# Two-layer trunk on one core: the sums of weight blocks formed in the second MLP sweep, the rotary tables beside the first gates, and softmax with priority

## The chip, the core and the metric

The kernel runs on one core of a Trainium2 chip. A core has a tensor engine (PE in the profile), a vector engine (DVE), a scalar engine (ACT), GpSimd (POOL), and a sync engine (SP) which here only issues transfers. Each engine takes its instructions in order from a queue of its own; semaphores make one engine wait for another. The metric is the device time in microseconds (us) of one execution, lower is better.

## The reference

One sequence of 1024 tokens, width 1024, passes two layers, all in float32. Layer 0 is an mLSTM mixer (8 heads, chunks of 128 tokens) and an MLP. Layer 1 is multi-head latent attention (8 heads, causal, rotary part of 64 columns) on keys and values made once from a low-rank latent, and an MLP. Every norm's gain and shift is modulated by vectors made from the condition `c` through large matrices (`ada_w`, `kv_ada_w`).

```python
def rope_tables(positions):
    half = B_ROPE // 2
    inv = ROPE_THETA ** (-jnp.arange(half, dtype=jnp.float32) / half)
    ang = positions.astype(jnp.float32)[..., None] * inv
    return jnp.cos(ang), jnp.sin(ang)
...
    for l in range(DEPTH):
        ada = cond @ ada_w[l] + ada_b[l]
        sh1, sc1, g1, sh2, sc2, g2 = jnp.split(ada, 6, axis=-1)
        h = modulate(rmsnorm(x, norm_g[l, 0]), sh1, sc1)
        if l < N_A:
            y = mlstm_mixer(h, a_w_in[l], a_gate_b[l], a_head_g[l], a_w_out[l])
        else:
            ...
            y = mla_mixer(h, b_w_q_a[j], b_q_latent_g[j], b_w_q_b[j], b_w_out[j],
                          k_nope, k_rope, v, cos, sin)
        x = x + g1[:, None, :] * rmsnorm(y, norm_g[l, 1])
        h = modulate(rmsnorm(x, norm_g[l, 2]), sh2, sc2)
        y = sqrelu_mlp(h, mlp_w1[l], mlp_w2[l])
        x = x + g2[:, None, :] * rmsnorm(y, norm_g[l, 3])
```

## The kernel before

**Products.** Each float32 operand is split into a rounded high part and a rest; a product is three matmuls (`mm3`, lines 280 to 282: high by high, high by rest, rest by high). A weight tile of 128x1024 is loaded by SP into one of four `raw` buffers; `wsplit` (lines 238 and 239) makes the high part on ACT and the rest on DVE, both in `ws` buffers. So each weight that PE takes has been a transfer, an ACT and a DVE instruction before.

**Order.** The program is traced as generators (`yield` marks a place where another strand may be woven in). A scheduler then sets the order on every engine by an estimate of its own; `prompt` (high priority) lets a piece go ahead of other ready work. `tc.issue_after` ties some DVE work to a point. What counts for this page is the resulting order on each engine, which is shown below where the change moves it.

**Buffers.** Tiles come from rings: `k4` (24 buffers of 128x1024), `hd` (8), `raw` (4), `ws` (8), `tmp` (3), `tmc` (6), and in the accumulators of PE `ps` (2), `pc` (2), `pm` (2 double ones). An instruction that takes a ring's next buffer waits until its last user is done.

**Stages,** by the trace: to 69 us the first half's input, its modulation and its query and key products; from 77 us the first gates (`gates_in`, `gates0`); up to about 510 us the mLSTM of both halves. Then the first MLP. It multiplies by blocks: the tokens are two halves, the weight `w1` is cut in halves along both sides, and seven block products stand in for eight. `Mlp.sweep1` (510 to 690 us) makes the products of the plain blocks, `sweep2` (690 to 893 us, `second`) those of sums and differences of blocks for the first half's results, and `sweep3` (from 893 us, `third`) the rest, beside `attention_first`, the attention of the first half. Afterwards come the second half's attention and the second MLP.

**Block sums.** For each of 16 column blocks `p_`, four 128x512 sums of `w1` blocks are wanted. `block_sums` makes all of them early: GpSimd's queue loads two tiles of 512 KB (line 2578), DVE makes four sums (lines 2583 to 2587), GpSimd's queue stores two tiles of 512 KB in the scratch tensor `t0` (lines 2585 and 2588). Five of the sixteen are woven into the first gates and the last query and key products (buffers `hd`), one more into what follows, and the rest into the second half's mLSTM. `second` reads two quarters of `t0` and one raw quarter of `w1`, and `third` reads the other two quarters. `self.made` says for which `p_` this holds: all sixteen of layer 0.

**Modulation and latents.** `ada_chunk` (lines 377 to 384) loads four tiles of 512 KB and adds them up on DVE, eight instructions of 128x512. In the first MLP a strand `behind(bg_latent(), 5)` walks beside the sweeps: the rest of these chunks, then `rope_tables` (sine and cosine of position by frequency, in two halves of 512 columns, range reduction on GpSimd, sines on ACT), then `latent_weights`, six weight tiles scaled and split. A `yield "wait"` ends the strand's turn until the next step of the sweep.

**First attention.** `attention_first` makes keys and query of a head (`kq`), the rotary part (`rot`), the values (`val`) and, in `scores` and `softmax` (lines 1832 to 1836: maximum, scaling on DVE, exponential on ACT, reciprocal and scaling on DVE), the weights, which PE then transposes (lines 1942 and 1953) for the product with the values.

## Time and profile before

| | |
|---|---|
| three runs | 2375.53, 2379.48, 2379.86 us; median 2379.48 |
| the profiled execution | 2381.42 us, of which the profile's span is 2379.6 |
| PE busy | 2298.5 us, 97% of the span |
| DVE busy | 1709.8 us, 72% |
| ACT busy | 1128.1 us, 47% |
| POOL busy | 160.7 us, 7% |
| moved by transfers | 465.37 MB, a mean of 196 GB/s |

The span is cut by stages in what follows. Of a stage, the reader wants four numbers: how long PE was not busy, at what clock it ran (1.00 is the full clock), how full DVE was, and how full the transfer engines were.

### The profile page before, as it was taken

Reading aid. Unit: us, or ns where it says so; the run is one execution under the profiler, and the core shown is the slowest. Engines: PE = TensorE matmul, PEld = TensorE weight load, DVE = VectorE, ACT = ScalarE, POOL = GpSimd, SP = SyncE. Lnnn points to the kernel's source line nnn. Section 1 sums busy time; section 2 is a strip of 40 time slices with the busy share of each in tenths; the row PEclk is TensorE's granted clock in tenths of the full one; section 3 lists DMA queues with packets and bytes.
Section 4 is the critical chain, followed back from the end, with each engine's and each line's share of the span. In section 5 each row is a group of like instructions: output and inputs, shape, how many; then the busy total and the mean of one; then the engine's idle time right before and its main releaser. Section 6 shows DMA issues by size and latency. Waiting matters only on the chain.

```text
span 2379.6 us, 32796 instructions
## 1 busy us (share of the span) xinstructions
PE 2298.5 (97%) x12042; PEld 1932.3 (81%) x12042; DVE 1709.8 (72%) x2771; ACT 1128.1 (47%) x1913; POOL 160.7 (7%) x271
## 2 busy tenths in 40 slices
PE   7899999999999999999899999999999999999998
PEld 5788797787778888777788778888888888999997
DVE  6576777889976766776674777766566478788776
ACT  3255433566435545543444555444444445555543
POOL 2100003103621100000000000000000000000000
PEclk9999999999999999999999999999999999999999
DMA  9862478956887967565576855683432452455432
GB/s 344 278 178 81 135 213 256 356 195 214 262 285 246 299 215 269 180 225 182 174 229 188 268 168 178 212 287 131 158 109 103 147 162 82 134 169 163 133 107 107
DMA packets 390594, 465.37 MB, mean 196 GB/s; under 512 B 27971, under 2 KB 265600, under 8 KB 390432
## 3 DMA queue, kind: packets, MB, share of 16 engines
q1 hardware_dynamic: 371136, 394.47, 52.7%
q0 software_dynamic: 19296, 68.79, 8.1%
q8 instruction: 95, 1.56, 0.3%
q14 instruction: 67, 0.55, 0.1%
HBM read 356.23 MB, written 106.95 MB: 195 GB/s over the span
## 4 chain that ended last, share of the span: by engine, by line
PE 66%; DVE 7%; DMA 5%; ACT 3%; issue 2%; SPq 1%; DVEq 0%; POOL 0%; ACTq 0%; POOLq 0%
PE ps L282 10%; PE ps L280 10%; PE ps L281 10%; PE pm L280 8%; PE pm L281 8%; PE pm L282 8%; PE pc L281 2%; PE pc L282 2%; PE pc L280 2%; DMA raw<-in_mlp_w_dram 2%; DVE tma L384 1%; PE pc L2023 1%; DVE wl L239 1%; DMA raw<-in_ada_w_dram 1%; DVE k L247 1%
## 5 line engine op out<-in xcount | busy, mean ns | idle before, releaser
L238 ACT CAST wh<-raw 128x1024 fp32r<-128x1024 f32 (+5 forms) x323 | 327.9, 1017 | 490.3 <-PE ps L281 170.3
L239 DVE TENSOR_TENSOR wl<-raw,wh 128x1024 fp32r<-128x1024 f32 (+5 forms) x323 | 383.2, 1188 | 242.2 <-ACT wh L238 198.5
L280 PE MATMUL ps<-k,wh 128*128 128x512 f32 (+1 forms) x1228 | 466.9, 380 | 5.5 <-ACT k L682 1.7
L282 PE MATMUL ps<-k,wl 128*128 128x512 f32 (+1 forms) x1228 | 460.1, 375 | 2.0 <-DVE wl L239 2.0
L281 PE MATMUL ps<-k,wh 128*128 128x512 f32 (+1 forms) x1228 | 459.8, 374 | 0.0
L280 PEld LDWEIGHTS ps<-k,wh 128*128 128x128 f32 x1228 | 232.0, 189 | 50.4 <-issue 2.6
L282 PEld LDWEIGHTS ps<-k,wl 128*128 128x128 f32 x1228 | 231.9, 189 | 45.0 <-DVE wl L239 3.4
L281 PEld LDWEIGHTS ps<-k,wh 128*128 128x128 f32 x1228 | 232.1, 189 | 40.9 <-issue 1.7
L247 DVE TENSOR_TENSOR k<-k,pm 128x512 f32<-128x512 f32 (+1 forms) x250 | 192.3, 801 | 79.2 <-PE pm L282 78.6
L280 PE MATMUL pm<-wh,hd 128*128 128x512 f32 x488 | 193.4, 396 | 3.0 <-ACT raw L1834 1.8
L281 PE MATMUL pm<-wl,hd 128*128 128x512 f32 x488 | 190.4, 390 | 0.0
L282 PE MATMUL pm<-wh,hd 128*128 128x512 f32 x488 | 190.4, 390 | 0.0
L384 DVE SCALAR_TENSOR_TENSOR tma<-raw,cond,tma 128x512 f32<-128x512 f32 x168 | 131.9, 785 | 17.0 <-DMA raw<-in_ada_w_dram 11.9
L280 PEld LDWEIGHTS pm<-wh,hd 128*128 128x128 f32 x488 | 91.7, 188 | 24.8 <-ACT raw L1834 4.5
L282 PEld LDWEIGHTS pm<-wh,hd 128*128 128x128 f32 x488 | 91.6, 188 | 19.7 <-DVE hd L494 0.5
L280 PE MATMUL pc<-k,wh 128*128 128x256 f32 (+1 forms) x316 | 103.4, 327 | 3.9 <-DVE hd L494 3.9
L1834 ACT ACTIVATE raw<-pm,sm 128x128 f32<-128x128 f32 (+3 forms) x64 | 47.5, 742 | 125.0 <-DVE sm L1833 122.8
L281 PEld LDWEIGHTS pm<-wl,hd 128*128 128x128 f32 x488 | 91.7, 188 | 18.4 <-issue 0.5
L280 PE MATMUL pm<-hd,wk 128*128 128x512 f32 x256 | 101.6, 397 | 2.2 <-ACT hd L493 2.2
L281 PE MATMUL pc<-k,wh 128*128 128x256 f32 (+1 forms) x316 | 103.4, 327 | 0.2 <-DVE k L494 0.2
L282 PE MATMUL pc<-k,wl 128*128 128x256 f32 (+1 forms) x316 | 103.2, 327 | 0.0
L281 PE MATMUL pm<-hd,wk 128*128 128x512 f32 x256 | 101.0, 395 | 1.9 <-DVE hd L494 1.9
(496 smaller groups left out, 4921.1 us busy)
## 6 DMA issues: line engine op xcount, KB each, us to landing
raw<-in_mlp_w_dram SPq DMA_DIRECT2D x144, 512.0 KB, 4.3
raw<-in_ada_w_dram SPq DMA_DIRECT2D x80, 512.0 KB, 5.2
raw<-in_mlp_w_dram SPq DMA_DIRECT2D x144, 256.0 KB, 4.4
raw<-in_a_w_in_dram SPq DMA_DIRECT2D x44, 512.0 KB, 5.2
lo<-wl POOLq DMA_DIRECT2D x32, 512.0 KB, 6.1
raw<-t SPq DMA_DIRECT2D x64, 256.0 KB, 5.1
wk<-lo SPq DMA_DIRECT2D x64, 256.0 KB, 4.3
k<-in_mlp_w_dram POOLq DMA_DIRECT2D x22, 512.0 KB, 9.8
```

The lines of the kernel that those rows point to most:

```text
L238: nc.scalar.copy(hi[:, :n], r[:, :n])
L239: i = nc.vector.tensor_sub(lo[:, :n], r[:, :n], hi[:, :n].bitcast(F32))
L247: return f(*a, **k)
L280: nc.tensor.matmul(o, lh, rh, start=start, stop=False)
L281: nc.tensor.matmul(o, lh, rl, start=False, stop=False)
L282: pe_last[0] = nc.tensor.matmul(o, ll, rh, start=False, stop=stop)
L384: nc.vector.scalar_tensor_tensor(acc, r[:, kk], cond[:, k : k + 1], acc, ALU.mult, ALU.add)
L1834: nc.scalar.activation(pr[:, :n], f, AF.Exp, bias=m, scale=SCALE, accum_out=l)
L2023: nc.tensor.transpose(pt[:, ts(2 * e + i, P)], u.prs[i][:, ts(b + e, P)], ident)
```

## The change

Three things change.

1. `block_sums`, `t0`, `order` and `made` go. `second` loads the two `w1` tiles of a block itself, and makes the three sums it needs on DVE and the fourth on GpSimd; a tile `s` with the two sums that `third` wants is stored by GpSimd's queue. `third` loads it as one tile.
2. `rope_tables` moves from the strand beside the sweeps to a place before `gates_in` of the first half. It works on all 1024 columns at once, in three `hd` tiles, with nearly all its arithmetic on GpSimd and its transfers on GpSimd's queue. It starts when the modulation's shift of the first norm is known (the one-column copy into `d`). `latent_weights` ends its turn two or three times a tile instead of once.
3. In `attention_first` the query's product takes its accumulator from `ps` instead of `pc`; `rot` goes ahead of the next even head's `kq`; `softmax` has priority in both attentions.

```diff
@@ class Mlp @@
-            self.made = not l and order or []
@@ second, load @@
-                if p_ in self.made:
-                    r = [raw(), raw()]
-                    nc.sync.dma_start(r[0][:, l_], t0[p_][:, 0:512])
-                    nc.sync.dma_start(r[1][:, l_], t0[p_][:, 1024:1536])
-                    nc.sync.dma_start(
-                        r[1][:, r_].rearrange("p (a b) -> p a b", b=P),
-                        wcols(self.w1, (p_ + NPR) * P, P, 4, 4),
-                    )
...
                 r = [raw(), raw()]
                 for i in range(2):
                     nc.sync.dma_start(
...
                 w = wsplit(r[1], 1024)
-                nc.vector.tensor_sub(o[:, r_], r[0][:, r_], r[0][:, l_])
+                nc.gpsimd.tensor_sub(o[:, r_], r[0][:, r_], r[0][:, l_])
                 nc.gpsimd.dma_start(self.s[p_], o)
@@ third, load @@
-                if p_ in self.made:
-                    nc.sync.dma_start(r[:, 0:512], t0[p_][:, 1536:2048])
-                    nc.sync.dma_start(r[:, 512:1024], t0[p_][:, 512:1024])
-                else:
-                    nc.sync.dma_start(r, self.s[p_])
+                nc.sync.dma_start(r, self.s[p_])
@@ latent_weights @@
-            yield "wait"
+            for _ in range(3 if b == 0 else 2):
+                yield "wait"
@@ scores, twice @@
-                softmax(st[:, e, :n], pr[:, e], n, e == 0)
+                prompt(softmax)(st[:, e, :n], pr[:, e], n, e == 0)
@@ attention_first @@
-            for t, k0, n, of, alloc in ((kt, 0, 2, hf.ckv, ps), (q, 2, 3, hf.cq, pc)):
+            for t, k0, n, of, alloc in ((kt, 0, 2, hf.ckv, ps), (q, 2, 3, hf.cq, ps)):
...
-                work += [kq(2 * p_ + 2), rot(p_ + 1), val(p_ + 1)]
+                work += [rot(p_ + 1), kq(2 * p_ + 2), val(p_ + 1)]
@@ rope_tables, new place @@
+        d, a, kf = hd(), hd(), hd()
+        pi = d.bitcast(I32)
+        nc.gpsimd.tensor_copy(d[:, 0:1], adac(0, SH1)[:, 7:8])
+        nc.gpsimd.dma_start(pi, positions.to_broadcast([P, S]))
+        nc.gpsimd.tensor_copy(a, pi)
+        nc.gpsimd.tensor_scalar(a, a, inv, None, ALU.mult)
+        yield
+        nc.gpsimd.tensor_scalar(kf, a, 1.0 / (2.0 * PI), MAGIC, ALU.mult, ALU.add)
+        nc.gpsimd.tensor_scalar_add(kf, kf, -MAGIC)
+        for part in TWO_PI_PARTS:
+            yield
+            nc.gpsimd.tensor_scalar(d, kf, -part, None, ALU.mult)
+            nc.gpsimd.tensor_add(a, a, d)
+        yield
+        nc.gpsimd.tensor_scalar(a, a, 3.1415925, -3.1415925, ALU.min, ALU.max)
+        nc.vector.scalar_tensor_tensor(kf, a, -1.0, a, ALU.mult, ALU.max)
+        nc.vector.tensor_scalar(kf, kf, -1.0, PI / 2, ALU.mult, ALU.add)
+        nc.scalar.activation(d, a, AF.Sin)
+        last = nc.scalar.activation(kf, kf, AF.Sin)
...
+        nc.gpsimd.tensor_scalar(d, d, sg, None, ALU.mult)
+        nc.gpsimd.dma_start(rope_d[1], d)
+        nc.gpsimd.dma_start(rope_d[0], kf)
@@ the program @@
-    pre = block_sums()
-    at_prep[0] = hd
-    drain(with_bg(with_bg(gates_in(hfs[0]), bgs, 1), pre, 1))
-    drain(with_bg(with_bg(qk_last(hfs[0]), bgs, 1), pre, 1))
+    drain(rope_tables())
+    drain(with_bg(gates_in(hfs[0]), bgs, 1))
+    drain(with_bg(qk_last(hfs[0]), bgs, 1))
...
-    drain(weave_n(with_bg(with_bg(main, bgs, 1.5), pre, 0.2), intra0(hfs[1]), 0.95))
+    drain(weave_n(with_bg(main, bgs, 1.5), intra0(hfs[1]), 0.95))
@@ bg_latent @@
         yield from bgs
-        yield from rope_tables()
```

The scheduler's order moves with this at three places. The first is DVE's queue at the end of the first query and key products. The names `hd` are the tiles of the block sums, `k` with L497 the rests of the modulated input that PE multiplies next, `wl` the rest of a weight. Before:

```order
L2381 SCALAR_TENSOR_TENSOR tmc_477<-k_14_148,mods,Cst 128x512
L2583 TENSOR_TENSOR hd_665<-hd_665 128x512
L2584 TENSOR_TENSOR hd_665<-hd_664,hd_665 128x512
L239 TENSOR_TENSOR wl_480<-raw_412,wh_479 128x1024
L2368 TENSOR_TENSOR ada<-pc_489,cols 128x4
L2586 TENSOR_TENSOR hd_664<-hd_665,hd_664 128x512
L2583 TENSOR_TENSOR hd_739<-hd_739 128x512
L2587 TENSOR_TENSOR hd_664<-hd_664 128x512
L497 SCALAR_TENSOR_TENSOR k_46_235<-tmc_475,ada,k_45_234 128x512
```

And with the change:

```order
L2327 SCALAR_TENSOR_TENSOR tmc_476<-k_14_147,mods,Cst 128x512
L239 TENSOR_TENSOR wl_479<-raw_411,wh_478 128x1024
L2314 TENSOR_TENSOR ada<-pc_488,cols 128x4
L497 SCALAR_TENSOR_TENSOR k_46_234<-tmc_474,ada,k_45_233 128x512
L497 SCALAR_TENSOR_TENSOR k_46_234<-tmc_476,ada,k_45_233 128x512
```

The block sums no longer stand between the modulation and the rests. GpSimd's queue has the rotary tables there in place of the block sums' transfers; these rows of it, with the change, show the memset of L730 (a tile that `gates0` fills for the decay matrices) behind a part of the tables:

```order
L2526 COPY hd_610<-ada 128x1
L2527 DMA hd_610<-in_positions_dram 128x1024
L625 MEMSET tmc_670 128x8x24
L2528 CAST hd_611<-hd_610 128x1024
L2529 TENSOR_SCALAR hd_611<-hd_611,inv 128x1024
```

```order
L2536 TENSOR_TENSOR hd_611<-hd_611,hd_610 128x1024
L730 MEMSET tmc_840 128x512
L2535 TENSOR_SCALAR hd_610<-hd_612 128x1024
L2536 TENSOR_TENSOR hd_611<-hd_611,hd_610 128x1024
L2535 TENSOR_SCALAR hd_610<-hd_612 128x1024
L2536 TENSOR_TENSOR hd_611<-hd_611,hd_610 128x1024
```

The second place is DVE in the second sweep. L247 are PE's results added up, L239 and L1030 (L1031 with the change) rests of weights, L1622 and L1624 (L1567 and L1569) the bias of a latent tile. Before, one step of the sweep:

```order
L247 TENSOR_TENSOR k_1218_7090<-k_1218_7090,ps_7225 128x512
L1624 SCALAR_TENSOR_TENSOR tma_7188<-raw_7186,ada,tma_7188 128x128 x5
L247 TENSOR_TENSOR k_1218_7090<-k_1218_7090,pc_7239 128x512
L239 TENSOR_TENSOR wl_7206<-raw_7186,wh_7205 128x1024
L1030 TENSOR_TENSOR wv_7218<-raw_7211,wv_7218 128x512
L247 TENSOR_TENSOR tmp_7255<-k_1218_7090,ps_7254 128x512
L239 TENSOR_TENSOR wl_7222<-raw_7212,wh_7221 128x1024
L239 TENSOR_TENSOR wl_7278<-raw_7274,wh_7277 128x1024
L494 TENSOR_TENSOR hd_7269<-tmp_7255,hd_7269 128x512
L247 TENSOR_TENSOR k_805_4784<-k_805_4784,pm_7282 128x1024
```

With the change, a step without a latent tile:

```order
L1026 TENSOR_TENSOR k_1202_7035<-raw_7031 128x512
L247 TENSOR_TENSOR k_1185_6932<-k_1185_6932,ps_7049 128x512
L1027 TENSOR_TENSOR raw_7031<-raw_7030,raw_7031 128x512
L1028 TENSOR_TENSOR raw_7030<-k_1202_7035,raw_7030 128x512
L247 TENSOR_TENSOR k_1185_6932<-k_1185_6932,pc_7063 128x512
L1031 TENSOR_TENSOR wv_7040<-raw_7030,wv_7040 128x512
L239 TENSOR_TENSOR wl_7044<-raw_7031,wh_7043 128x1024
L239 TENSOR_TENSOR wl_7102<-raw_7098,wh_7101 128x1024
L247 TENSOR_TENSOR tmp_7079<-k_1185_6932,ps_7078 128x512
L494 TENSOR_TENSOR hd_7093<-tmp_7079,hd_7093 128x512
L247 TENSOR_TENSOR k_776_4665<-k_776_4665,pm_7106 128x1024
```

Three sums (L1026 to L1028) stand among the accumulations; a latent tile's work now stands in every second step, and before it stood in consecutive ones. The third place is ACT in the first attention, around the second exponential of a unit with 512 keys (L1834, L1780 with the change). Before:

```order
L1834 ACTIVATE raw_9295,sm_9309<-pm_9294,sm_9308 128x384
L493 CAST k_1604_9331<-pc_9341 128x512
L238 CAST wh_9326<-raw_9323 128x640
L1834 ACTIVATE raw_9295,sm_9317<-pm_9294,sm_9316 128x512
L974 ACTIVATE u_1563_9134<-u_1563_9134 128x512
```

With the change:

```order
L1780 ACTIVATE raw_9172,sm_9186<-pm_9171,sm_9185 128x384
L493 CAST k_1579_9208<-ps_9218 128x512
L1780 ACTIVATE raw_9172,sm_9194<-pm_9171,sm_9193 128x512
L238 CAST wh_9203<-raw_9200 128x384
L974 ACTIVATE u_1538_9013<-u_1538_9013 128x512
```

The cast of a weight that has to be loaded first now stands behind the exponential.

More of the change, by code (lines that the diff above doesn't have):

```diff
@@ L1858, in scores @@
                 pr = raw()
-                softmax(st.rearrange("p a b -> p (a b)")[:, :n], pr, n, e == 0)
+                prompt(softmax)(st.rearrange("p a b -> p (a b)")[:, :n], pr, n, e == 0)
                 prs.append(pr)
@@ L2628 @@
             )
-    pre = block_sums()
-    at_prep[0] = hd
-    drain(with_bg(with_bg(gates_in(hfs[0]), bgs, 1), pre, 1))
-    drain(with_bg(with_bg(qk_last(hfs[0]), bgs, 1), pre, 1))
+    drain(rope_tables())
+    drain(with_bg(gates_in(hfs[0]), bgs, 1))
+    drain(with_bg(qk_last(hfs[0]), bgs, 1))
     x1 = load_x1()
-    at_prep[0] = k4
-    for _ in range(2):
-        next(pre, None)
     drain(weave(with_bg(v_in(hfs[0]), bgs, 1), intra0(hfs[0]), 2.5))
```

71 lines of the change are left out of this document (12 added, 59 removed).

## The prediction

> **What bounds the kernel now.** I read the page first, then PE's busy time by stages, then PE's longest waits, then the engines around each wait. The page says that PE is nearly always busy, and that the transfer engines are full in places (first row the vector of 40 slices, then totals).
>
> ```profile
> span 2379.6 us, 32796 instructions
> PE 2298.5 (97%) x12042; PEld 1932.3 (81%) x12042; DVE 1709.8 (72%) x2771; ACT 1128.1 (47%) x1913; POOL 160.7 (7%) x271
> DMA  9862478956887967565576855683432452455432
> ```
>
> So a change that leaves PE's products as they are can win only PE's 81 us of idle time (2379.6 - 2298.5) and the time that PE runs below its full clock. The stages show where both lie; the columns are the stretch, its length, each engine's busy time, PE's granted clock, the transfer engines' share and GB/s.
>
> ```profile
> 40.00:90.00 50.00, 36.90 (x179) 30.66 (x172) 28.97 (x43) 12.77 (x25) 11.24 (x21) 0.80 0.98 336
> 380.00:480.00 100.00, 90.17 (x413) 72.81 (x412) 82.42 (x145) 48.96 (x87) 23.82 (x41) 0.95 1.04 336
> 590.00:690.00 100.00, 89.65 (x380) 70.72 (x380) 92.70 (x111) 44.36 (x59) 52.38 (x46) 0.97 0.83 276
> 690.00:900.00 210.00, 210.00 (x934) 173.61 (x933) 140.27 (x206) 100.05 (x157) 23.99 (x47) 1.00 0.79 255
> 1020.00:1200.00 180.00, 162.65 (x837) 135.70 (x836) 123.22 (x246) 72.66 (x144) 2.95 (x13) 0.96 0.61 192
> ```
>
> Idle time: 13.1, 9.8, 10.4, 0 and 17.4 us. The first two stages hold block sums and full transfer engines, the third the rotary tables, the fifth the first attention; the fourth, the second sweep, has no gap and is where the change puts work.
>
> **The first products and gates (40 to 90 us).** DVE waits for a block sum's transfer, and the rest that PE needs (L497) stands behind the sums; PE then waits, and later once more for the gates' weights.
>
> ```profile
> 42.72 0.69 DVE L2583 TENSOR_TENSOR hd<-hd 128x512 f32<-128x512 f32 x1 [1.74 <-DMA hd<-in_mlp_w_dram]
> ...
> 48.35 0.69 DVE L2583 TENSOR_TENSOR hd<-hd 128x512 f32<-128x512 f32 x1 [1.35 <-DMA hd<-in_mlp_w_dram]
> 48.97 0.68 DVE L2587 TENSOR_TENSOR hd<-hd 128x512 f32<-128x512 f32 x1
> 49.57 0.74 DVE L497 SCALAR_TENSOR_TENSOR k<-tmc,ada,k 128x512 fp32r<-128x512 f32 x1
> ```
> ```profile
> 47.22 0.80 PE L280 MATMUL pm<-k,wh 128*128 128x512 f32 x1 [3.05 <-ACT k L496]
> 50.36 0.80 PE L281 MATMUL pm<-k,wh 128*128 128x512 f32 x1 [2.35 <-DVE k L497]
> ...
> 77.10 0.59 PE L280 MATMUL ps<-wh,k 128*128 128x272 f32 x1 [7.71 <-ACT k L247]
> ```
> ```profile
> 72.42 1.65 ACT L238 CAST wh<-raw 128x816 fp32r<-128x816 f32 x2 [15.24 <-DMA raw<-in_a_w_in_dram]
> ```
>
> The block tiles on GpSimd's queue (ten here, 22 later; KB each and median us to landing):
>
> ```profile
> k<-in_mlp_w_dram POOLq DMA_DIRECT2D x22, 512.0 KB, 9.8
> ...
> hd<-in_mlp_w_dram POOLq DMA_DIRECT2D x10, 512.0 KB, 10.1
> ```
>
> After each gap PE ran at half clock for some us, as these short stretches show.
>
> ```profile
> 77.00:83.40 6.40, 6.30 (x28) 6.30 (x29) 6.37 (x12) 0.99 (x5) 1.84 (x7) 0.51 0.97 342
> 47.00:56.00 9.00, 6.43 (x14) 4.75 (x15) 7.65 (x13) 3.21 (x5) 1.07 (x2) 0.50 1.03 350
> 392.00:400.00 8.00, 7.13 (x42) 6.04 (x43) 5.74 (x11) 1.25 (x3) 3.45 (x5) 0.67 1.03 328
> 455.00:470.00 15.00, 10.65 (x39) 7.88 (x38) 15.00 (x23) 12.90 (x22) 1.05 (x7) 0.89 1.05 349
> ```
>
> Without block sums DVE reaches L497 after one weight rest instead of five further instructions. *Term A*: the gaps are 3.05 + 2.35 = 5.4 us, the clock costs 6.43 x 0.50 = 3.2 us, 8.6 in all; some 2 us of the gap belong to the weight and the modulation themselves, so I take -6 (bounds -8.6 and 0). *Term B*: the gates' weights come late because the queue is full: ten block tiles, 5 MB, and as much in stores share it. The gap is 7.7 us and the clock costs 6.30 x 0.49 = 3.1, 10.8 in all; I take -9 (bounds -10.8 and -3, if the weights' buffers rather than the traffic hold them).
>
> **The second half's mLSTM (380 to 480 us).** Ten pairs of block tiles pass here at a share of 1.04. One wait is plainly theirs: a sum waits for its tile, and L858, which PE needs, is behind it.
>
> ```profile
> 391.43 0.69 DVE L2583 TENSOR_TENSOR k<-k 128x512 f32<-128x512 f32 x1 [1.39 <-DMA k<-in_mlp_w_dram]
> 392.04 0.68 DVE L858 TENSOR_TENSOR tmc<-pm,sm 128x512 f32<-128x512 f32 x1
> ```
> ```profile
> 392.87 1.09 PE L884 MATMUL pc<-ident,tmc 128*128 128x128 f32 x4 [5.48 <-DVE tmc L858]
> ```
>
> *Term C*: 5.5 us of gap and 7.13 x 0.33 = 2.4 us of clock go. Of the 4.35 us of gap and 1.2 us (10.65 x 0.11) of clock at 455 to 470, where DVE is full with norms too, I take half, 2.8: -10.6 (bounds -13.4 and -5).
>
> **The rotary tables out of the sweeps.** GpSimd's arithmetic slows DVE. Same instructions, first at 140 to 360 us without it, then at 575 to 670 beside it; then GpSimd's own, from 575 to 720.
>
> ```profile
> L239 DVE TENSOR_TENSOR wl<-raw,wh 128x1024 fp32r<-128x1024 f32 x30 | 36.6, 1221 | 24.9 <-ACT wh L238 15.5 <-PE pc L884 4.4 <-PE ps L553 3.1
> L384 DVE SCALAR_TENSOR_TENSOR tma<-raw,cond,tma 128x512 f32<-128x512 f32 x40 | 29.9, 747 | 5.9 <-DMA raw<-in_ada_w_dram 5.4
> ...
> L384 DVE SCALAR_TENSOR_TENSOR tma<-raw,cond,tma 128x512 f32<-128x512 f32 x34 | 31.9, 939 | 1.3 <-DMA raw<-in_ada_w_dram 0.7
> L239 DVE TENSOR_TENSOR wl<-raw,wh 128x1024 fp32r<-128x1024 f32 x15 | 21.2, 1415 | 1.4 <-ACT wh L238 1.3
> ...
> L1548 POOL TENSOR_SCALAR tmc<-tmc 128x512 f32<-128x512 f32 x14 | 24.3, 1739 | 2.1 <-DVE k L494 1.0
> L1549 POOL TENSOR_TENSOR tmc<-tmc,tmc 128x512 f32<-128x512 f32 x14 | 19.6, 1398 | 0.7
> ```
>
> L384 gives back 34 x 0.19 = 6.5 us, L239 15 x 0.19 = 2.9, so DVE falls from 93% to about 80% in that stage. *Term D*: idle 10.35 us and 89.65 x 0.03 = 2.7 us of clock; the chunks of modulation stay, so I take 60%, -7.8 (bounds -13 and 0).
>
> In the new place, *term G*: 13 single-source and 7 two-source GpSimd instructions at double width, 13 x 2 x 1.74 + 7 x 2 x 1.40 = 65 us at the crowded rate. They start once the shift is known, near 45 us (some 5 before the L497 above), and should end by 110 to 120. DVE there is busy 29 of 50 us; a fourth more (939/747) fits into its idle time. ACT reaches the first sine after two of four rounds of exponentials, here the last of the second:
>
> ```profile
> 129.86 1.14 ACT L769 ACTIVATE tmc<-pc,gc 128x128 f32<-128x128 f32 x4 [0.93 <-PE pc L765]
> ```
>
> That place, 131 us, comes some 15 us sooner now, near 116. If GpSimd is late, ACT's queue stands with the values' copies behind the sine, and PE's two accumulators fill; ACT's wait of 15.24 us above cost PE 10.8. I take +2 (bounds 0 and +10.8). DVE's absolute value of the angle waits for GpSimd too, with the accumulations of modulation behind it, which have a chunk's time to spare. The memset of L730 stands behind a part of the tables, but the row that it clears is wanted only by `gates0`, after the gates' transposes: at 0. The seven transfers on GpSimd's queue replace twenty of the block sums' there; ten leave SP's, which is not what PE waits for: at 0.
>
> **The second sweep (690 to 900 us).** Each of 16 steps gains three DVE sums, priced as the nearest instruction of that shape:
>
> ```profile
> L1030 DVE TENSOR_TENSOR wv<-raw,wv 128x512 fp32r<-128x512 f32 x12 | 8.2, 684 | 0.0
> ```
>
> 16 x 3 x 0.684 = 33 us, on 140 of 210: DVE at 82%. GpSimd's difference, 16 x 1.4 = 22 us, slows DVE by a fourth of that, 6 us: 85%. Traffic: a step loads 1.25 MB instead of 1.0 and stores 0.5 MB more, 16 x 0.75 = 12.6 million bytes in 210 us, 60 GB/s on 255; by bytes the share goes from 0.79 to 0.98. Before, single tiles of latents made peaks here; they are now spread over twice the steps. *Term E*: PE has no idle time to give back here, so the gain side is 0; the loss side is the loss of 590 to 690, where DVE was at 93%: 10.35 per 100 us, +22. DVE stays below that and the transfers come close to full, so I take +7.
>
> SP loses 32 issues in all. GpSimd's queue loses 64 block transfers and gets 16 stores of `s`; each waits for that queue's own difference only. In the third sweep one load replaces two: 0.
>
> **The first attention (1020 to 1200 us).** PE's waits there on the softmax chain:
>
> ```profile
> PE pc L1953 <- DVE raw L1836: 3.6, 3, 1.8
> PE pc L1942 <- DVE raw L1836: 3.0, 1, 3.0
> PE pc L1953 <- DVE sm L1833: 2.8, 2, 1.7
> ```
> ```profile
> 1050.00 0.73 ACT L238 CAST wh<-raw 128x640 fp32r<-128x640 f32 x1 [2.27 <-DMA raw<-in_b_w_q_b_dram]
> 1050.63 0.69 ACT L1834 ACTIVATE raw<-pm,sm 128x512 f32<-128x512 f32 x1
> ```
>
> An exponential stood behind a cast that waited 2.27 us for a weight; priority turns them. What then comes late are casts of weights, with a step in hand. *Term F*: 9.4 us of named waits; I take half, -5. Bounds: -15.9 with all the clock (162.65 x 0.04 = 6.5), and +6 if the query, now in `ps`, keeps the sweep's products from their two accumulators.
>
> **Sum.** -6 - 9 - 10.6 - 7.8 + 2 + 7 - 5 = -29.4. The profiled execution took 2381.4 us (span 2379.6 and 1.8 around it), which gives 2352; it stands 1.9 above the median, so 2350 against 2379.5. The likeliest case's own range, with the terms off by half here and there, is 2336 to 2364.
>
> **Rivals.** *The second sweep gets as bad as the stage before it* (E at +22): 2365. For it: a share near 0.98. Against: from 750 to 840 the latents raised traffic to 285 GB/s and PE lost nothing. 0.17.
> *The early gaps stay in part,* since buffers hold the weights: half of A to D, 16.7 us less gain: 2367. Against it: DVE's order, quoted above. 0.07.
> *GpSimd holds the first gates* (G at +10.8): 2359. By the rows a DVE instruction loses 0.19 us beside GpSimd. The Trainium skill, "SBUF — State Buffer", section "Who interferes with whom", says that GpSimd and a DVE instruction with two inputs from SBUF lock each other out for a whole instruction. By it each of 20 GpSimd instructions of some 3 us would hold DVE for half its length, 30 us in a stage with 21 idle, which is about that price. The rows so far show a fifth of a microsecond, not halves of an instruction. 0.06.
> *Slower:* the extra tile `o` of each step takes a `k4` buffer until GpSimd's queue has stored it, and SP, which already waits for such buffers, issues the next weights late.
>
> ```profile
> SPq L1027 <- DMA u<-k: 22.7, 11, 5.6
> ```
>
> SP waited 2.1 us a time there (22.7/11) and 5.6 at most. The other terms give 36.4 us, so it decides from 36.4/16 = 2.3 us lost by PE in a step; at 3.6, the middle between that mean and the longest, the time is 2401. Against it: PE lost nothing to these waits so far. 0.12.
>
> **Chances.** The forecast 0.58, the rivals 0.17, 0.07, 0.06 and 0.12. About 0.2% (4.8 us) is what a measurement of this kernel tells from no change. The first four cases end faster, but for their upper edges (0.05): faster 0.83, same 0.05, slower 0.12. The range reaches from 2330, below the forecast's own by some of the better bounds, to 2378, above the first three rivals.
>
> **What would show it.** Right: no gap of 5 us before the gates' first product or before L884's transposes; 40 to 90 and 380 to 480 us with a share well under 1; DVE under 85% from 590 to 690; PE full in the second sweep, with three 0.7 us sums a step; exponentials without a weight's cast ahead. Wrong: PE gaps in the second sweep with SP waiting for buffers or DVE at a sum's transfer; ACT standing at the first sine.

## The result, and the profile after

The changed kernel takes 2338.9 us (median of 4 runs, 2336.3 to 2339.3) against 2378.6 us (4 runs beside them). The ratio is 0.983, 95% interval 0.982 to 0.985. The forecast was 2350 us. The profiled execution took 2336.3 us, with a span of 2334.1 us; before it was 2379.6 us.

These are the span, the totals and the vector of 40 slices of the changed kernel's page.

```profile
span 2334.1 us, 32606 instructions
PE 2283.2 (98%) x12042; PEld 1922.5 (82%) x12042; DVE 1704.7 (73%) x2749; ACT 1126.0 (48%) x1911; POOL 146.3 (6%) x231
DMA  9452464657899888566686754874434452455432
```

PE's idle time fell from 81.1 to 50.9 us. Of the transfers' full blocks the one near 400 us is gone, the one at the start is down to the first slice, and there is one long block, the sweeps.

Next are the stages of the changed kernel that answer to those of the prediction (they lie earlier by what was saved before them), and one stage of the kernel before that the prediction did not show. The columns are as there: busy time of PE, PEld, DVE, ACT, POOL, then PE's clock, the transfers' share, GB/s.

```profile
40.00:90.00 50.00, 49.09 (x285) 41.21 (x278) 32.87 (x33) 20.02 (x37) 39.38 (x22) 1.00 0.70 232
90.00:130.00 40.00, 32.28 (x233) 28.36 (x232) 37.78 (x59) 16.28 (x34) 15.10 (x7) 0.87 0.33 100
360.00:460.00 100.00, 99.68 (x494) 81.69 (x493) 72.08 (x126) 58.21 (x102) 0.79 (x8) 1.00 0.52 160
550.00:650.00 100.00, 97.64 (x439) 80.00 (x438) 83.79 (x115) 40.09 (x55) 9.37 (x17) 1.00 0.83 275
650.00:860.00 210.00, 199.63 (x864) 160.33 (x863) 160.53 (x236) 86.64 (x143) 50.05 (x69) 0.99 0.90 288
980.00:1160.00 180.00, 174.90 (x924) 146.95 (x925) 140.87 (x275) 84.48 (x166) 2.62 (x12) 1.00 0.68 216
```
```profile
90.00:130.00 40.00, 37.49 (x255) 31.62 (x253) 29.60 (x54) 14.81 (x34) 2.86 (x4) 1.00 0.71 227
```

What a stage loses is its length less PE's busy time times the clock; for 40 to 90 us before, 50 - 36.90 x 0.80 = 20.5 us. Worked out so for every row:

| stage (before) | loss before | loss after | difference | terms |
|---|---|---|---|---|
| 40 to 90 | 20.5 | 0.9 | -19.6 | A and B, -15 |
| 90 to 130 | 2.5 | 11.9 | +9.4 | G, +2 |
| 380 to 480 | 14.3 | 0.3 | -14.0 | C, -10.6 |
| 590 to 690 | 13.0 | 2.4 | -10.6 | D, -7.8 |
| 690 to 900 | 0 | 12.4 | +12.4 | E, +7 |
| 1020 to 1200 | 23.9 | 5.1 | -18.8 | F, -5 |

The differences sum to -41.2, and the two spans differ by 45.5; the rest is spread over stages that the table leaves out. Every sign came out as foretold, and no size did: the gains are larger than taken, and so are both losses. The two new losses show as PE's longest waits of the changed kernel (us in total, times, longest).

```profile
PE pc L743 <- DVE tmc L712: 6.1, 1, 6.1
PE ps L282 <- DVE wv L1031: 3.8, 4, 1.3
PE ps L280 <- ACT wv L1030: 3.6, 2, 2.1
...
PE ps L280 <- DVE tmp L247: 2.8, 2, 2.1
```

L743 are the transposes of the first gates. L1030 and L1031 are the head and the rest of the second sweep's new weight, the sum that DVE makes there now.

**What the rotary tables do to DVE.** These are some of DVE's instructions of the first gates' chain (start, length), and then GpSimd's of the same time.

```profile
88.22 2.76 DVE L704 SCALAR_TENSOR_TENSOR tmc<-tmc,tmc 8x512 f32<-8x512 f32 x1
90.91 1.51 DVE L705 SCALAR_TENSOR_TENSOR tmc<-tmc,tmc 8x512 f32<-8x512 f32 x1
92.45 0.68 DVE L706 TENSOR_TENSOR tmc<-tmc,tmc 8x512 f32<-8x512 f32 x1
93.17 4.26 DVE L709 TENSOR_TENSOR_SCAN tmc<-ones,tmc 8x128 f32<-8x128 f32 x4
97.46 0.68 DVE L712 TENSOR_TENSOR tmc<-tmc,tmc 8x512 f32<-8x512 f32 x1
98.68 0.15 DVE L719 TENSOR_TENSOR mcol<-tmc,tmc 8x1 f32<-8x1 f32 x1
99.37 2.15 DVE L719 TENSOR_TENSOR mcol<-tmc,tmc 8x1 f32<-8x1 f32 x1
```
```profile
87.99 2.45 POOL L2536 TENSOR_TENSOR hd<-hd,hd 128x1024 f32<-128x1024 f32 x1
90.52 3.09 POOL L2535 TENSOR_SCALAR hd<-hd 128x1024 f32<-128x1024 f32 x1
93.70 2.34 POOL L2536 TENSOR_TENSOR hd<-hd,hd 128x1024 f32<-128x1024 f32 x1
96.12 2.77 POOL L2535 TENSOR_SCALAR hd<-hd 128x1024 f32<-128x1024 f32 x1
98.97 2.54 POOL L2536 TENSOR_TENSOR hd<-hd,hd 128x1024 f32<-128x1024 f32 x1
```

L719 adds eight numbers. It took 0.15 us once, and 2.15 us when it started inside a GpSimd sum: it ended at 101.52, and GpSimd's sum ended at 101.51. L704, 0.68 us in the kernel before, ended 0.54 us after GpSimd's sum that ran at its start. Beside GpSimd's products (L2535) it is otherwise: L706 and L712, which have two inputs as L719 has, kept their 0.68 us inside one, and L705, which began 0.39 us into one, took 1.51 us in place of 0.67. Added up from L696 to the last L719, DVE's instructions took 11.9 us more than the same ones in the kernel before, and PE stood 6.1 us until L712 was done.

### The profile page after: what moved, and what is told of

It reads as the page before. It is cut to its first block, busy times and chain, and to the rows that moved or that the text cites. A ratio compares the mean times of both kernels' runs of the same rounds, so it can differ in the third digit from the quotient of the medians.

```text
span 2334.1 us, 32606 instructions
## 1 busy us (share of the span) xinstructions
PE 2283.2 (98%) x12042; PEld 1922.5 (82%) x12042; DVE 1704.7 (73%) x2749; ACT 1126.0 (48%) x1911; POOL 146.3 (6%) x231
## 4 chain that ended last, share of the span: by engine, by line
PE 77%; DVE 9%; DMA 8%; ACT 2%; issue 2%; SPq 1%; DVEq 0%; ACTq 0%
PE ps L280 13%; PE ps L282 12%; PE ps L281 12%; PE pm L280 9%; PE pm L281 9%; PE pm L282 8%; DMA raw<-in_mlp_w_dram 5%; PE pc L281 2%; PE pc L282 2%; PE pc L280 2%; DVE wl L239 1%; DMA raw<-in_a_w_in_dram 1%; PE pc L1969 1%; DVE k L247 1%; PE pm L1774 1%
## 5 line engine op out<-in xcount | busy, mean ns | idle before, releaser
L239 DVE TENSOR_TENSOR wl<-raw,wh 128x1024 fp32r<-128x1024 f32 (+5 forms) x323 | 382.6, 1187 | 210.2 <-ACT wh L238 185.3
L280 PE MATMUL ps<-k,wh 128*128 128x512 f32 (+1 forms) x1252 | 475.7, 380 | 5.6 <-DVE tmp L247 2.8
L282 PE MATMUL ps<-k,wl 128*128 128x512 f32 (+1 forms) x1252 | 467.9, 374 | 0.3 <-DVE wl L239 0.3
L281 PE MATMUL ps<-k,wh 128*128 128x512 f32 (+1 forms) x1252 | 467.7, 374 | 0.1
L280 PEld LDWEIGHTS ps<-k,wh 128*128 128x128 f32 x1252 | 235.9, 188 | 51.6 <-DVE tmp L247 3.6
L281 PEld LDWEIGHTS ps<-k,wh 128*128 128x128 f32 x1252 | 236.0, 188 | 41.9 <-issue 1.4
L247 DVE TENSOR_TENSOR k<-k,pm 128x512 f32<-128x512 f32 (+1 forms) x250 | 192.4, 801 | 62.7 <-PE pm L282 62.1
L384 DVE SCALAR_TENSOR_TENSOR tma<-raw,cond,tma 128x512 f32<-128x512 f32 x168 | 126.9, 755 | 23.3 <-DMA raw<-in_ada_w_dram 14.2
L281 PE MATMUL pm<-hd,wk 128*128 128x512 f32 x256 | 100.0, 391 | 1.7 <-DVE hd L494 1.7
L280 PE MATMUL pm<-hd,wk 128*128 128x512 f32 x256 | 100.8, 394 | 0.6 <-ACT hd L493 0.6
L1780 ACT ACTIVATE raw<-pm,sm 128x128 f32<-128x128 f32 (+3 forms) x64 | 47.5, 743 | 110.8 <-DVE sm L1779 107.2
L280 PE MATMUL pm<-hd,wh 128*128 128x512 f32 x256 | 99.5, 390 | 0.9 <-DVE tma L384 0.9
L282 PE MATMUL pm<-hd,wl 128*128 128x512 f32 x256 | 99.7, 390 | 0.5 <-DVE wl L239 0.5
L282 PE MATMUL pm<-hd,wk 128*128 128x512 f32 x256 | 99.8, 390 | 0.0
```

The lines of the kernel that those rows point to most:

```text
L239: i = nc.vector.tensor_sub(lo[:, :n], r[:, :n], hi[:, :n].bitcast(F32))
L247: return f(*a, **k)
L280: nc.tensor.matmul(o, lh, rh, start=start, stop=False)
L281: nc.tensor.matmul(o, lh, rl, start=False, stop=False)
L282: pe_last[0] = nc.tensor.matmul(o, ll, rh, start=False, stop=stop)
L384: nc.vector.scalar_tensor_tensor(acc, r[:, kk], cond[:, k : k + 1], acc, ALU.mult, ALU.add)
```

## The experiments

All ratios are against the kernel before, with their 95% intervals.

### The three parts apart

Three kernels take the change by its parts: part 1 alone (rotary tables and first attention as before), the change without part 2, and the change without part 3. The edits undo the change's diff part by part; the core of the last two:

```diff
@@ parts 1 and 3 @@
-    drain(rope_tables())
+        yield from rope_tables()
...
-            for _ in range(3 if b == 0 else 2):
-                yield "wait"
+            yield "wait"
@@ parts 1 and 2 @@
-                prompt(softmax)(st[:, e, :n], pr[:, e], n, e == 0)
+                softmax(st[:, e, :n], pr[:, e], n, e == 0)
...
-            for t, k0, n, of, alloc in ((kt, 0, 2, hf.ckv, ps), (q, 2, 3, hf.cq, ps)):
+            for t, k0, n, of, alloc in ((kt, 0, 2, hf.ckv, ps), (q, 2, 3, hf.cq, pc)):
...
-                work += [rot(p_ + 1), kq(2 * p_ + 2), val(p_ + 1)]
+                work += [kq(2 * p_ + 2), rot(p_ + 1), val(p_ + 1)]
```

Part 1 alone has both of these edits.

> The kernel before with part 1 alone: block sums made in the second sweep, rotary tables still in the strand beside the sweeps, the first attention as it was. Theory (the early block sums cost what terms A to C say, and the second sweep costs some 12 us, as PE's idle time and clock from 650 to 860 us of the changed kernel read): -25.6 + 12, so 2366 against 2379, and 40 to 90 us and the second half's mLSTM without gaps. Rival 1 (the sums and the rotary tables, now both beside the sweeps, hurt each other): the sweeps lose 20 us or more, 2374 to 2380. Rival 2 (the gain of the early stages comes from elsewhere): the gaps of 3.05, 2.35, 7.7 and 5.5 us stay.

> The changed kernel with part 2 undone: rotary tables in the strand beside the sweeps again, one turn's end per latent tile. Theory 1 (GpSimd's tables lengthen DVE's chain of the first gates from about 18 to 24 us to the first result, and PE pays some 9 us of gap and clock for it; in the strand they cost the 10 us of term D): no 6.1 us gap before the transposes of the gates, a gap of some 10 us in the sweeps instead, time within 4 us of the changed kernel's 2339. Rival (the chain is slow for another reason, such as its own order): the gap of 6 us stays and the time is 2347 to 2352.

> The changed kernel with part 3 undone: the query's accumulator from the other pool, keys before the rotation, softmax without priority. Theory 1 (all of PE's idle time and lost clock of the first attention belongs to this part, 12 us of busy time and 6 us of clock between the two profiles): 2354 to 2358, with PE's waits on the softmax chain of 3 us and the clock at 0.96 back. Theory 2 (term F, the named waits only): 2344. Rival (the gain there is that of other traffic and timing, not of this part): 2339 to 2341.

| kernel | us | ratio, interval |
|---|---|---|
| part 1 alone | 2350.9 | 0.988 (0.987 to 0.990) |
| parts 1 and 3 | 2336.8 | 0.983 (0.981 to 0.984) |
| parts 1 and 2 | 2355.8 | 0.990 (0.989 to 0.992) |
| all three | 2338.9 | 0.983 (0.982 to 0.985) |

Part 1 is worth 27.5 us by itself (2378.4 before in those runs), more than the 13.6 expected here. Part 3 adds 14.1 us to it, and 16.9 us where part 2 is in as well. Part 2 gains nothing: with it the time is 2.1 us longer beside part 3 and 4.9 us longer without it, and in both pairs the intervals overlap. The stages of the kernel with parts 1 and 3 show why:

```profile
90.00:130.00 40.00, 40.00 (x313) 35.76 (x312) 33.56 (x64) 20.35 (x54) 0.00 (x0) 1.00 0.59 177
460.00:650.00 190.00, 180.88 (x780) 145.53 (x779) 167.26 (x213) 99.26 (x141) 72.21 (x67) 0.98 0.70 234
```

With the tables in the strand, the first gates lose nothing, and 460 to 650 us lose 190 - 180.88 x 0.98 = 12.7 us. With the tables in the new place 460 to 650 us lose 2.4 us and the gates 11.9. The loss has moved, as theory 1 of that kernel said.

### Softmax's priority alone

```diff
-                prompt(softmax)(st[:, e, :n], pr[:, e], n, e == 0)
+                softmax(st[:, e, :n], pr[:, e], n, e == 0)
```

(twice, in the changed kernel)

> The changed kernel with only softmax's priority undone; the query's accumulator and the order of the rotation stay. The whole of part 3 is worth 14 to 17 us (2350.9 to 2336.8, and 2355.8 to 2338.9). Theory 1 (term F as told: an exponential behind a cast that waits for its weight): nearly all of it comes back, 2350 to 2356, with an exponential behind a cast again. Theory 2 (the two reorderings of the first attention, not the priority): 2339 to 2343. In between, the parts share it.

It took 2347.2 us, 0.986 (0.984 to 0.989), and its runs lie wide apart (2339.8 to 2352.7), so that its interval just touches the changed kernel's. Both causes share: some 8 us go with the priority, and the rest of part 3's 14 to 17 with the query's accumulator and the rotation's place. PE's busy time from 980 to 1160 us is 169.42 us at a clock of 0.98, between the 163.67 at 0.96 without part 3 and the changed kernel's 174.90 at 1.00.

PE's waits say which part does what. These are the two longest from 980 to 1200 us (us in total, times, longest), first without part 3, then without the priority alone.

```profile
PE pc L1888 <- DVE raw L1782: 3.7, 1, 3.7
PE pc L1899 <- DVE raw L1782: 3.6, 3, 1.8
```
```profile
PE pc L280 <- DVE hd L494: 6.9, 3, 5.6
PE pc L1899 <- DVE raw L1782: 1.8, 1, 1.8
```

All waits on the softmax chain (L1779 and L1782) are 9.2 us without part 3, 3.0 us without the priority and 2.1 us in the changed kernel. So the accumulator and the rotation's place took most of them away, by one profile of each kernel. What went with the priority is the wait for a rest that DVE makes (`hd`, L494): 6.9 us without it, 2.0 in the changed kernel.

### The rotary tables earlier, and on DVE

First, the start gate is removed.

```diff
-        nc.gpsimd.tensor_copy(d[:, 0:1], adac(0, SH1)[:, 7:8])
```

> The changed kernel with the rotary tables' start gate removed (the one-column copy from the modulation's shift): GpSimd starts on them as soon as the positions have landed, some 35 us sooner, and should be through before the first gates' chain on DVE begins at 80 us. Theory 1 (GpSimd's instructions hold DVE's, 0.47 us ones for 2.6 and 0.15 us ones for 2.15): the chain takes some 11 us less, no gap of 6.1 us, and the sums of modulation before 45 us, which wait for transfers, hide what they lose: 2329 to 2332. Rival 1 (DVE's modulation before the first product is what sets the start): the first product comes 5 to 10 us later and the time is 2335 to 2345. Rival 2 (the chain is slow by itself): the gap stays, 2339.

It took 2346.9 us, 0.987 (0.985 to 0.989): slower than the changed kernel. From 40 to 90 us it loses 50 - 46.48 x 0.93 = 6.8 us, against 0.9, and the gates hardly gain (10.8 us from 90 to 130, against 11.9). The tables did not start where the edit wanted them, since the buffer for the positions came free at 32.5 us only:

```profile
32.51 0.57 POOL L2526 DMA_DIRECT2D hd<-in_positions_dram  x1 [21.18 <-DVE tmc L2289]
39.75 1.04 POOL L2527 CAST hd<-hd 128x1024 f32<-128x1024 int32 x1 [6.68 <-issue]
```

So they ran some 10 us earlier, and then the memset of L730, which waits for the gates' products, stood ahead of the last five of them in GpSimd's queue:

```profile
85.73 0.53 POOL L730 MEMSET tmc<- 128x512 f32 x1 [6.37 <-PE pc L640]
```

They ran beside the chain's first half after all, and ended at 98.5 us. The chain's second half had its plain lengths (L709 1.36 us, L719 0.15). The run does not answer what a start at 10 us would do, but it shows the chain's instructions long only while GpSimd works.

Then the same arithmetic, at the changed kernel's place, on DVE:

```diff
-        nc.gpsimd.tensor_copy(a, pi)
-        nc.gpsimd.tensor_scalar(a, a, inv, None, ALU.mult)
+        nc.vector.tensor_copy(a, pi)
+        nc.vector.tensor_scalar(a, a, inv, None, ALU.mult)
...
-            nc.gpsimd.tensor_scalar(d, kf, -part, None, ALU.mult)
-            nc.gpsimd.tensor_add(a, a, d)
+            nc.vector.scalar_tensor_tensor(a, kf, -part, a, ALU.mult, ALU.add)
```

> The changed kernel with the rotary tables' arithmetic at the same place on DVE instead of GpSimd (a product and a sum as one instruction; only the start copy and the last product by the sign stay on GpSimd). Theory 1 (two-source instructions on GpSimd hold DVE for their whole length, so it is the lock and not the amount of work that costs): DVE gets 13 instructions of about 0.8 to 1.5 us into its idle time before 80 us, the first gates' chain takes some 11 us less, no gap of 6.1 us before the gates' transposes: 2327 to 2331. Rival 1 (any work ahead of the chain delays it; rests of weights wait behind the tables): the gap stays in part, 2335 to 2342. Rival 2 (the chain's length does not come from the tables): 2339.

It took 2329.0 us, 0.979 (0.977 to 0.980), 9.9 us less than the changed kernel, and faster than both kernels of this comparison by more than the intervals. DVE has more to do and its chain is short again:

```profile
89.54 0.68 DVE L704 SCALAR_TENSOR_TENSOR tmc<-tmc,tmc 8x512 f32<-8x512 f32 x1
94.25 0.15 DVE L719 TENSOR_TENSOR mcol<-tmc,tmc 8x1 f32<-8x1 f32 x1
```
```profile
90.00:130.00 40.00, 38.92 (x305) 35.13 (x304) 34.65 (x67) 19.07 (x51) 0.00 (x0) 1.00 0.57 180
```

The wait of 6.1 us is gone. What PE had waited for was GpSimd at work beside DVE's chain, not the amount of work ahead of the gates.

### The second sweep

The fourth sum on DVE:

```diff
-                nc.gpsimd.tensor_sub(o[:, r_], r[0][:, r_], r[0][:, l_])
+                nc.vector.tensor_sub(o[:, r_], r[0][:, r_], r[0][:, l_])
```

> The changed kernel with the second sweep's fourth sum on DVE instead of GpSimd. Between 640 and 880 us PE loses some 12 us, half of it waiting for the rests and heads of the sweep's weights (L1030, L1031); L1031 takes 0.99 us where the same instruction took 0.68 before. Theory 1 (GpSimd's sum holds L1031, which PE waits for): L1031 back to 0.68 us, 16 x 0.3 = 4.8 us less on the chain, 2334 to 2336. Rival (DVE's time is what counts there, and 16 x 0.68 us more is worse): 2340 to 2345.

2339.4 us, 0.983 (0.982 to 0.985): no change. L1031 went back from 0.99 to 0.68 us, so GpSimd's sum had lengthened it, and PE's waits for L1030 and L1031 halved (3.6 us between 600 and 880 us, against 7.4), but one for a weight's rest came in their place:

```profile
PE pm L282 <- DVE wl L239: 4.7, 2, 4.1
PE ps L280 <- ACT wv L1030: 2.1, 2, 1.8
PE ps L282 <- DVE wv L1031: 1.5, 2, 1.0
```

The sums and splits without priority; the loads keep theirs:

```diff
+                with tc.high_priority(PRIO):
+                    r = [raw(), raw()]
...
-            return prompt(load), hid
+            return load, hid
```

> The changed kernel with the second sweep's sums and splits without priority; the loads keep theirs. DVE stood 32.7 us between 640 and 880 us at L1026, the first sum, for a tile that had not landed, with accumulations behind it that PE wants. Theory 1 (a sum at the wrong place in DVE's queue is the loss): L1026's wait falls by more than half and PE gets 5 us or more back: 2330 to 2335. Rival 1 (the tiles themselves come late, the queue's order only shows it): PE's waits stay, 2337 to 2341. Rival 2 (the sums come later still, and PE waits for the weights made from them): 2345 or more.

2341.3 us, 0.984 (0.982 to 0.985). DVE's wait at the first sum stayed (32.0 us, against 32.7), since the scheduler left the sums about where they were. The run tells nothing of theory 1.

Two of the sums left out:

```diff
-                nc.vector.tensor_sub(r[1][:, l_], r[0][:, l_], r[1][:, l_])
-                nc.vector.tensor_sub(r[0][:, l_], o[:, l_], r[0][:, l_])
```

> The changed kernel with two of the second sweep's sums (L1027 and L1028) left out: the products there use the weight tiles as loaded, so the output is not the reference's; all transfers and the other two sums stay. Between 600 and 860 us PE loses some 13 us. Theory 1 (the two raw tiles of a step are one loop: issue, landing after 7 to 8 us, three sums, the cast and the rest, which frees them for the next issue; 704.1 to 716.8 us in one step, as long as PE's own step): 1.4 us or more out of each round, PE's loss there falls to 5 us or less, 2330 to 2334. Rival 1 (the traffic, share 0.90, which stays as it is): PE's loss stays, 2337 to 2340. Rival 2 (DVE's load: 22 us less of it): same time as theory 1, but then DVE's waits for landed tiles would be short.

2340.0 us, 0.983 (0.980 to 0.985): no change, and from 650 to 860 us PE is busy for 200.76 us (199.63 in the changed kernel), though DVE fell from 160.5 to 142.5. Neither DVE's load nor the three sums in a row is the cause.

The second tile in another buffer, on the kernel with the tables on DVE:

```diff
-                r = [raw(), raw()]
+                r = [raw(), k4()[:, :1024]]
```

> The kernel with the rotary tables on DVE (2329.0 us) with the second sweep's second weight tile in a k4 buffer instead of a raw one: same sums, same traffic, one raw buffer more for the other loads. Theory 1 (the raw buffers' loop paces the second sweep): SyncE's waits for L1031 and L239 before L1020 get shorter, PE's loss of some 12 us between 600 and 860 us halves: 2321 to 2325. Rival 1 (traffic or DVE): no change, 2327 to 2331. Rival 2 (k4 buffers are the scarcer ones, held by stores of s and u): slower, 2332 or more.

2335.8 us, 0.982 (0.979 to 0.984): 6.8 us slower than 2329.0. SyncE's waits before L1020 shrank, and it waited for a raw buffer before the next weight instead (L260, 76 us in all between 640 and 880 us). PE's loss from 650 to 860 us did not fall (210 - 200.69 x 0.99 = 11.3 us, against 10.5).

Eight of the sixteen steps' sums made between 120 and 330 us, by the kernel before's own `block_sums` on `k4` tiles, on the kernel with the tables on DVE:

```diff
-    in_turn(og0(hfs[0], hdv), chunks0(hfs[0]), n1)
+    pre = block_sums()
+    in_turn(with_bg(og0(hfs[0], hdv), pre, 2), chunks0(hfs[0]), n1)
```

> The kernel with the rotary tables on DVE (2329.0 us) with the sums of eight of the sixteen steps made between 120 and 330 us beside the first half's chunks, where the transfers' share is 0.28 to 0.75 and DVE at 61 to 76%, and loaded in the second sweep as in the kernel before. Theory 1 (the second sweep's loss goes with the number of steps that make sums; where the traffic has room, early sums cost nothing): half of 12 us back, 2322 to 2325. Rival 1 (sums anywhere on DVE's queue make PE wait, as in terms A and C): new gaps between 120 and 330 us, 2329 to 2338. Rival 2 (the second sweep's loss does not come from its sums): 2328 to 2330.

2336.8 us, 0.982 (0.979 to 0.984). Theory 1 and rival 1 held at once. The second sweep's loss halved, from 10.5 to 210 - 204.51 = 5.5 us, and the early stages gave back 14 us of idle time:

```profile
90.00:130.00 40.00, 34.00 (x262) 30.11 (x260) 31.30 (x62) 13.16 (x35) 2.93 (x4) 1.00 0.66 216
130.00:360.00 230.00, 220.29 (x1428) 189.25 (x1428) 169.67 (x353) 102.12 (x221) 19.61 (x33) 0.98 0.64 193
```
```profile
201.73 0.69 DVE L2545 TENSOR_TENSOR k<-k 128x512 f32<-128x512 f32 x1 [5.01 <-DMA k<-in_mlp_w_dram]
206.01 0.69 DVE L858 TENSOR_TENSOR tmc<-pm,sm 128x512 f32<-128x512 f32 x1
```
```profile
206.85 1.09 PE L884 MATMUL pc<-ident,tmc 128*128 128x128 f32 x4 [6.04 <-DVE tmc L858]
```

That is term C again in another place and with the transfers at a share of 0.64: a sum waits 5.01 us for its tile, L858 stands behind it, and PE waits 6.04 us at L884.

Last, no tile `s`: the third sweep loads the two `w1` tiles itself (on the kernel with the tables on DVE).

```diff
@@ second, load @@
-                nc.gpsimd.tensor_sub(o[:, r_], r[0][:, r_], r[0][:, l_])
-                nc.gpsimd.dma_start(self.s[p_], o)
@@ third, load @@
-                nc.sync.dma_start(r, self.s[p_])
+                for i in range(2):
+                    nc.sync.dma_start(
+                        r[i].rearrange("p (a b) -> p a b", b=P),
+                        wcols(self.w1, (p_ + NPR * i) * P),
+                    )
...
+                nc.vector.tensor_add(r[1][:, r_], r[1][:, l_], r[1][:, r_])
+                nc.vector.tensor_sub(r[0][:, l_], r[1][:, r_], r[0][:, l_])
+                nc.vector.tensor_sub(r[1][:, l_], r[0][:, r_], r[0][:, l_])
```

> The kernel with the rotary tables on DVE (2329.0 us) without the tile s: the second sweep neither makes its fourth sum nor stores s, and the third sweep loads both w1 tiles again and makes what it needs with three sums on DVE. The second sweep moves 0.5 MB of some 2.25 less a step, the third 0.5 MB more. Two runs before left the second sweep's loss as it was, with 22 us less of DVE's sums in one, and GpSimd's sum gone in the other; eight steps without sums halved it. Theory 1 (the second sweep is paced by its transfers, share 0.89): PE's loss between 600 and 860 us, some 12 us, falls to 6 or less there; the third sweep, among the first attention at a share of 0.6 to 0.85, gives some back, 2322 to 2332. Rival 1 (what paces it is the loads' own time to landing, 7 us after issue, whatever else moves): the loss stays at 10 to 12 and the third sweep adds to it, 2332 to 2340. Rival 2: the third sweep loses more than the second gains, above 2332 with the second sweep's loss halved.

2376.1 us, 0.998 (0.997 to 0.999): nearly all of the gain is lost, most of it behind the second sweep (from 980 to 1100 us PE is busy for 105.98 of 120 us at 0.96). For the second sweep the answer is plain:

```profile
650.00:860.00 210.00, 197.80 (x857) 159.38 (x856) 151.84 (x235) 86.22 (x143) 20.77 (x38) 0.99 0.78 242
```

The share fell from 0.89, in the kernel with the tables on DVE, to 0.78, and PE's loss there did not fall (210 - 197.80 x 0.99 = 14.2 us, against 10.5). The volume of the transfers is not the cause.

### What the trace says of the second sweep

The loss goes with the number of steps that make sums, since eight fewer halved it, but neither DVE's time for them, nor GpSimd's sum, the raw buffers or the volume sets it. What is left is when PE waits. In the changed kernel its seven gaps after 690 us, 9.4 of the 11.5 us of gaps of 0.4 us and more from 640 to 880, fall beside the work on one of the six latent tiles or within ten microseconds behind it; the tiles stand in every second step. One of them, on ACT, DVE and PE:

```profile
786.15 0.40 ACT L1573 ACTIVATE raw<-raw,mods 128x128 f32<-128x128 f32 x1 [0.46 <-DVE tma L1569]
787.45 0.79 ACT L1573 ACTIVATE raw<-raw,mods 128x128 f32<-128x128 f32 x2 [0.90 <-DVE tma L1569]
788.27 1.04 ACT L238 CAST wh<-raw 128x1024 fp32r<-128x1024 f32 x1
789.22 0.61 ACT L1030 CAST wv<-raw 128x512 fp32r<-128x512 f32 x1
```
```profile
785.17 0.69 DVE L1028 TENSOR_TENSOR raw<-k,raw 128x512 f32<-128x512 f32 x1
```
```profile
789.89 0.50 PE L280 MATMUL ps<-k,wv 128*128 128x512 f32 x1 [1.44 <-ACT wv L1030]
```

L1028, the sum, is done at 785.86. Its cast L1030, which PE needs, starts at 789.22. Ahead of it in ACT's queue stand the scalings of the latent tile (L1573), each waiting for DVE to have read its block (L1569), and one more cast. The kernel with two sums left out has its later gaps at the tiles' spacing of some 30 us too (at 789.13, 818.39 and 849.22), and so has the one without `s` (at 785.40, 816.83 and 846.99).

Two runs have the latent tiles at other places. In part 1 alone and in parts 1 and 3, where `latent_weights` ends its turn once a tile, they stand in consecutive steps, from 716 to 797 us, and the last four steps with sums (812 to 846 us) have none beside them. There PE's gaps end with the tiles: with parts 1 and 3 those after 700 us are at 743.42, 761.12, 762.34 and 806.32 us, 4.9 us in all, and none of 0.4 us or more follows up to 880; part 1 alone has them within half a microsecond of these places. From 690 to 880 us the gaps add up to 5.9 and 6.6 us in these two, against 9.4, though the share is higher (0.94, against 0.89). So the gaps follow the latent tiles. What the tiles cost is not measured: no run left them out or put their work behind the sums' casts.

## Why the prediction was right, and where it was wrong

**A and B** (-15, measured -19.6). Right in mechanism: DVE reaches L497 without block sums, and PE's gaps of 3.05 and 2.35 us became 0.61 and 0.29. The weights' gap of 7.7 us is gone and the clock is 1.00 (with part 1 alone too), so it went with the block sums and their traffic, and the buffers that B allowed for did not hold it. I kept back some 5 us (-19.6 against -15) for causes that weren't there.

**C** (-10.6, measured -14.0). Right; the step "I take half" for 455 to 470 us was too low, since that half went too. The run with eight early pairs brought the mechanism back at another place.

**D** (-7.8, measured -10.6). Right; in the strand, with parts 1 and 3, the tables cost 12.7 - 2.4 = 10.3 us. DVE fell to 84%; the step's own numbers give 83, not the 80 that it says. Of the 40% kept back for the chunks of modulation, half was lost there.

**G** (+2, measured +9.4). Wrong in its mechanism. The failed step is "a fourth more (939/747) fits into its idle time". Two things were wrong with it. The 0.19 us were a mean; the spread of the same 34 instructions in the kernel before (minimum, median and maximum, in ns) says something else:

```profile
L384 DVE SCALAR_TENSOR_TENSOR tma<-raw,cond,tma x34: 735/752/1772, 585.1 to 664.1; 128x512 f32<-128x512 f32 x34
```

Half of them lost next to nothing and the worst one 1.02 us, in a stage where GpSimd's instructions are 1.4 to 1.8 us long. At double width they are about 2.5 to 3 us long. And idle time of DVE in a stage is no cover for a chain in which each instruction waits for the last. The place I feared, ACT at the first sine, saw no wait: the tables were done at 102.6 us and the sine ran at 122.9. The rival with a chance of 0.06, GpSimd holding the first gates, had the mechanism and nearly the price (+10.8). The Trainium skill, "SBUF — State Buffer", section "Who interferes with whom", states the rule: an exclusive lock, held for a whole instruction. The trace agrees beside GpSimd's sums, with L719 at 2.15 us in place of 0.15. Beside its products it does not: L706 and L712 kept their 0.68 us. What I made of the rule, 30 us, was too much: DVE's chain lost 11.9 us, 9.1 of it in the four instructions that met a sum (L696, L704, L709, L719).

**E** (+7, measured +12.4). Right in sign, wrong in mechanism. The step was the one that scaled the loss by DVE's load and the transfers' share. DVE stood at 76% and the share at 0.90, both under what was taken (85% and 0.98), and the loss was larger; the runs then took away two of DVE's three sums, GpSimd's sum and 0.5 MB a step, and each of these took off 1.1 us or nothing; only eight steps without any sums halved it (5.5 us). The prediction saw the latent tiles "spread over twice the steps" as a relief of traffic, and did not ask whose queue they stand in. The gaps stand where latent tiles and sums meet in the queues of ACT and DVE, and they moved with the tiles in two runs; how much of the 12.4 us that makes stays open.

**F** (-5, measured -18.8 by the stage, -14.1 and -16.9 by the runs). Right in sign, and beyond its better bound of 15.9 in two of three measures, but right in mechanism for a part only. The step that failed is "priority turns them": the named waits on the softmax chain went for the most part with the query's accumulator and the rotation's place, which the prediction knew only as a danger (+6). In the changed kernel exponentials of 512 keys still stand behind casts that waited 1.02 and 2.78 us for a weight (at 1055.60 and 1107.05). The priority is worth some 8 us, by a wait (L494) that the prediction did not name. And the clock, 6.5 us, stood in the bound and not in the sum; all of it came back.

**The slower rival** (SP late for buffers) did not come: SyncE does wait for stores of `s` and `u` before L1025 (13.9 and 13.3 us), but PE's waits there are the ones above, and not 2.3 us a step. The run without `s` shows SyncE's waits for `u` growing to 55.5 us there. (The rival's own sum had a slip: the middle between 2.1 and 5.6 us is 3.8, not 3.6, which gives 2404 and not 2401.)

So the forecast was 11 us too high because the gains were taken too small, by some 25 us in A to D and F, which the 13 us of under-priced losses in G and E partly hid. That the sum came so near is in part luck: the errors of the terms add up to 37 us and ran against each other.

## What to carry to other kernels

Price work on GpSimd by the length of its single instructions against a dependent chain on DVE, and read minimum, median and maximum of what runs beside it, not the mean. A wait that goes can take lost clock of its stage with it, so cost both: here 0.80, 0.95, 0.97 and 0.96 became 1.00, though 10.5 us of short waits in one second sweep left the clock at 1.00. Before a loss in a busy stage is put down to traffic or load, look at which steps lose and what stands ahead of the late instruction in its queue.

## What was not expected of the hardware

A GpSimd `tensor_scalar` with one operation took nearly three times one with two, on the same tile of the changed kernel:

```profile
L2535 POOL TENSOR_SCALAR hd<-hd 128x1024 f32<-128x1024 f32 x7 | 20.8, 2965 | 0.5
L2531 POOL TENSOR_SCALAR hd<-hd 128x1024 f32<-128x1024 f32 x1 | 1.0, 1049 | 0.1
```

L2535 multiplies, L2531 multiplies and adds. In the kernel before it was 1.74 against 0.63 us at half the width. And the 19 instructions of the tables that filled GpSimd from 50.6 to 102.6 us took DVE, in the faster kernel, 12 instructions and 12.0 us.
